# Query of head 0: from the first stage's loop to the head of the projection stream

## The chip, the cores and the metric

The kernel runs on one core of one Trainium2 chip. The metric is the time of one execution in device microseconds; below, the profile of one execution stands beside the median of three timed runs.

## The reference

One trunk layer over 512 latent tokens of width 1024, with 256 context tokens ahead of them. It is cut here to what the change touches:

```
mod = silu(c) @ w_ada + b_ada                       # six parts: shift, scale, gate, twice
h   = rmsnorm(x) * g * (1 + scale) + shift          # for latent and context tokens
z   = h @ w_in + b_in                               # x, B, C | q, k, v, r, low-rank decays | gates A, B
o   = gated linear attention over heads 0..3, forwards and backwards (q, k, v, decays)
y   = sigmoid(gate_a) * conv branch + sigmoid(gate_b) * (rmsnorm(o) * silu(r)) @ w_gla_out
x   = x + gate1 * (y @ w_o)
x   = x + gate2 * relu(h2 @ w_up)^2 @ w_down        # h2 is x, normalized and modulated again
out = rmsnorm(x)
```

The query of a head is 128 of the columns of `z`. With eight blocks of 128 input channels it is a sum over eight products; in this kernel each product of two f32 matrices is made of three matmuls on rounded halves (`mm3`, line 137: high x high, high x low, low x high).

## The kernel before

Weights are loaded as f32 into raw buffers (line 106; `NRAW` is 4, of 512 KB each), and `split` (ACT casts the high half, DVE subtracts to get the low half) fills a pair of `hi` and `lo` tiles, five pairs in rotation. `weights` (line 126) does both for one block.

**The first stage** (lines 421 to 464) runs over the eight channel blocks, called steps 0 to 7 here. A step needs the shift and scale of its block, which themselves come from a product: `ada_raw` (line 186) loads 1 MB of `w_ada` for a block in two raw buffers (four DMAs on SP), `mod_products` makes 16 small matmuls of them (`ps_mod`), ACT copies the result (`sm`), four tiny matmuls turn it into columns (`ps_mc`), and DVE adds biases (`mod`). Four transposes bring the tokens of the block to channels by tokens (`ps_xt`); ACT scales and shifts them twice, once rounded (`hh`) and once not (`h_f`), and DVE takes the difference (`hl`). Then come the products of the step: 12 matmuls for the keys of four heads (`ps_k`, weights `wk` of 256 KB, split into `wkh` and `wkl`) and three for the query of head 0 (`ps_q0`). The sums stay in PSUM over all eight steps: four banks for the keys, one for the low-rank decays, one for this query; two of the eight banks are left for `ps_mod`, `ps_mc` and `ps_xt`. `ps_mod` of a step is computed in the step before it, and the loads run two steps ahead. The query's weights take one raw buffer and one pair of `hi` and `lo` at the start of the stage (line 429).

**The steady stream** follows. `Stream` (line 531) holds a plan of weight blocks in the order of use and loads up to three ahead of the one in use, five pairs at most. `projections` (line 891) takes them: eight blocks for the values (`ps_v`, six groups of 24 matmuls for each half, with the context's tokens, keys and decays in between), then the query of head 1, the convolution's inputs and the other queries, the gates. Attention runs interleaved with it: `all_attention` is advanced once for each `yield` of `projections`; it waits for `q_t[h]`, and first starts after the first `yield`, which stands behind the first group of `ps_v`.

**What sets the order.** In the set-up, before line 431, instructions of ACT, DVE and TensorE keep the order in which they are written. In the loop and the stream a planner orders the instructions of each engine by their priority (their place in the program, with parts moved up by `tc.high_priority`) and by when it thinks that their inputs and buffers are ready. Each engine then runs its list in order. DMAs of weights are issued by SP, in one list as well, so a load that waits for a raw buffer holds up all loads behind it.

The profile names tiles without numbers at the end; `ps_q0` appears there as `ps_q`, `ps_k0` to `ps_k3` as `ps_k`, the tiles of line 429 as `r_q`, `h_q` and `l_q`.

Of the kernel before, what the change touches and what calls it, by code (L numbers as in the profile page):

```python
# [20 lines left out]
KT = D // P  # L21
# [29 lines left out]
def hybrid_block_kernel(  # L51
# [40 lines left out]
    def blk(name, dt=F32):  # L92
        return bp.tile([P, 512], dt, tag="blk", name=name)
# [9 lines left out]
    def psum(name):  # L103
        return pp.tile([P, 512], F32, tag="ps", name=name)
# [21 lines left out]
    def weights(name, src):  # L126

        raw = raw_tile("r_" + name)
        a, b = src.shape[1], src.shape[2]
        nc.sync.dma_start(out=raw.rearrange("p (a b) -> p a b", a=a), in_=src)  # L130
        hi = wp.tile([P, 1024], F32R, tag="hi", name="h_" + name)
        lo = wp.tile([P, 1024], F32R, tag="lo", name="l_" + name)
        split(raw, hi, lo, name == "up")
        latest[0] = lo
        return hi.rearrange("p (a b) -> p a b", a=a), lo.rearrange("p (a b) -> p a b", a=a)

    def mm3(ps, lh, ll, rh, rl, start, stop, late=False, more=False):


        pe.matmul(ps, lh, rh, start=start, stop=False, skip_group_check=more)  # L140
        for l, r in ((ll, rh), (lh, rl)) if late else ((lh, rl), (ll, rh)):
            pe.matmul(ps, l, r, start=False, stop=stop and r is (rl if late else rh), skip_group_check=more)

    def cols(w, c0, n=P):
        return w[:, c0:c0 + n].rearrange("(k p) c -> p k c", p=P)

    def rows(w, k0, c0):
        return w[k0 * P:(k0 + 2) * P, c0:c0 + 512].rearrange("(k p) c -> p k c", p=P)
# [272 lines left out]
    warm(5)  # L421
    ps_k = [psum(f"ps_k{h}") for h in range(HEADS)]
    ps_lr = psum("ps_lr")
    ps_q0 = psum("ps_q0")
    latent_h(0, pst)
    key_raws[1] = key_raw(1)
    mod_w[1] = [ada_raw(1, q) for q in range(2)]
    normalized(x_tok, r_x, 0, P)
    wq = weights("q0", cols(w_in, C_Q))
    key_weights(1)  # L430
    Engine.ordered = False
    for m in range(MT):
# [2 lines left out]
    for k in range(KT):  # L435
        if k == 3:
            constants()
        if k + 2 < KT:
            key_raws[k + 2] = key_raw(k + 2)
            mod_w[k + 2] = [ada_raw(k + 2, q) for q in range(2)]  # L440
            key_weights(k + 2)
        elif k + 2 == KT:
            for m in range(MC):
                t = (blk(f"c_{m}_0"), blk(f"c_{m}_1"))
                for hf in range(2):
                    nc.sync.dma_start(out=t[hf], in_=ctx[m * P:(m + 1) * P, hf * 512:(hf + 1) * 512])
                c_tok.append(t)
        st, sp_ = k == 0, k == KT - 1
        if k % 4 == 3:
            low_rank_products(ps_lr, h_f32, k - 3)  # L450
        if k == KT - 1:
            lr_parts = low_rank_parts(ps_lr, SEQ)
        for h in range(HEADS):
            if h == (k == 0) and k + 1 < KT:
                sm = mod_rows(k + 1)
            if h == 2 and 0 < k < KT - 1:
                with tc.high_priority(offset=60):
                    mod_cols(k + 1, sm)
                    latent_h(k + 1)
            mm3(ps_k[h], wk[k][0][:, h * P:(h + 1) * P], wk[k][1][:, h * P:(h + 1) * P], h_hi[k], h_lo[k], st, sp_, st)  # L460
        mm3(ps_q0, wq[0][:, k, :], wq[1][:, k, :], h_hi[k], h_lo[k], st, sp_)
        if k == 0:
            with tc.high_priority(offset=60):
                mod_cols(1, sm)
                latent_h(1)
# [87 lines left out]
            self.live -= 1  # L553
            self.pump()

    plan = [("v", rows(w_in, 2 * g, C_V + 512 * hf)) for hf in range(2) for g in range(KT // 2)]
    plan.append(("q", cols(w_in, C_Q + DK)))
    for j in range(KT):
        plan += [("xa", cols(w_in, C_XA + j * P)), ("c", cols(w_in, C_C + j * P)), ("b", cols(w_in, C_B + j * P))]
# [34 lines left out]
    v_lat = [[None, None] for _ in range(MT)]  # L594
    v_ctx = [[None, None] for _ in range(MC)]
    lr_lat = low_rank("l", low_rank_sum(lr_parts, SEQ), SEQ)
    q_t[0] = blk("q_0")
    dve.tensor_scalar(out=q_t[0], in0=ps_q0, scalar1=cb(24), scalar2=float(DK) ** -0.5, op0=ALU.add, op1=ALU.mult)
    for h in range(HEADS):
        k_lat.append(blk(f"k_{h}"))  # L600
        act.activation(out=k_lat[h], in_=ps_k[h], func=AF.Identity, bias=cb(28 + h))
# [287 lines left out]
    ya, gate, gb, og = [], [], [], []  # L889

    def projections():

        for hf in range(2):
            vb = blk(f"vb_{hf}")
            nc.gpsimd.dma_start(out=vb, in_=b_in[C_V + 512 * hf:C_V + 512 * hf + 512].partition_broadcast(P))
            wv = [ws.take("v") for _ in range(KT // 2)]
            for m in range(MT + MC):
                if hf == 0 and m == 2:
                    context_h()
                if hf == 0 and m == MT:  # L900
                    ps = psum("ps_lrc")[:, 0:CTX]
                    for k0 in (0, 4):
                        low_rank_products(ps, c_f32, k0)
                    lr_parts_c = low_rank_parts(ps, CTX)
                    for h in range(HEADS):
                        ps = psum("ps_kc")[:, 0:CTX]
                        for k in range(KT):
                            mm3(ps, wk[k][0][:, h * P:(h + 1) * P], wk[k][1][:, h * P:(h + 1) * P], c_hi[k], c_lo[k], k == 0, k == KT - 1)
                        if h % 2 == 0:
                            kb = blk(f"kc_{h}")  # L910
                        k_ctx.append(kb[:, CTX * (h % 2):CTX * (h % 2) + CTX])
                        act.activation(out=k_ctx[h], in_=ps, func=AF.Identity, bias=cb(28 + h))
                        if h == 0:
                            lr_ctx.append(low_rank("c", low_rank_sum(lr_parts_c, CTX), CTX))
                        if h % 2 == 0:
                            yield
                ps = psum("ps_v")
                for k in range(KT):
                    hh, hl = (h_hi[k], h_lo[k]) if m < MT else (c_hi[k], c_lo[k])
                    ms = slice((m % MT) * P, (m % MT + 1) * P)  # L920
                    mm3(ps, hh[:, ms], hl[:, ms], wv[k // 2][0][:, k % 2, :], wv[k // 2][1][:, k % 2, :], k == 0, k == KT - 1)
                    if m == MT + MC - 1 and k % 2:
                        ws.free()
                vt = (kblk if m < MT else blk)(f"v_{m}_{hf}")
                dve.tensor_tensor(out=vt, in0=ps, in1=vb, op=ALU.add)
                (v_lat if m < MT else v_ctx)[m % MT][hf] = vt
                yield

        def query(h):
            ps = project("q")  # L930
            q_t[h] = blk(f"q_{h}")
            dve.tensor_scalar(out=q_t[h], in0=ps, scalar1=cb(24 + h), scalar2=float(DK) ** -0.5, op0=ALU.add, op1=ALU.mult)

        query(1)
        yield
        for j in range(KT):
            xa = blk("xa")
            ps = project("xa")
            act.activation(out=xa, in_=ps, func=AF.Identity, bias=cb(j))
            yield  # L940
            ps = project("c")
            dve.scalar_tensor_tensor(out=xa, in0=ps, scalar=cb(16 + j), in1=xa, op0=ALU.add, op1=ALU.mult)
            t = blk("cv")
            act.activation(out=t, in_=xa, func=AF.Copy, scale=cb(64 + 8 + j))
            u3 = xa.rearrange("p (r w) -> p r w", w=GRID_W)
            t3 = t.rearrange("p (r w) -> p r w", w=GRID_W)
            dve.scalar_tensor_tensor(out=t3[:, :, 1:], in0=u3[:, :, :-1], scalar=cb(64 + j), in1=t3[:, :, 1:], op0=ALU.mult, op1=ALU.add)
            dve.scalar_tensor_tensor(out=t3[:, :, :-1], in0=u3[:, :, 1:], scalar=cb(80 + j), in1=t3[:, :, :-1], op0=ALU.mult, op1=ALU.add)
            yield
            ps = project("b")  # L950
            dve.scalar_tensor_tensor(out=t, in0=ps, scalar=cb(8 + j), in1=t, op0=ALU.add, op1=ALU.mult)
            new = kblk if j in (5, 6) else blk
            ya.append((new(f"yah_{j}", F32R), new(f"yal_{j}", F32R)))
            split(t, *ya[j])
            yield
            if j in (1, 4):
                query(2 if j == 1 else 3)
                yield
        for j in range(KT):
            ps = project("ga")  # L960
            gate.append(blk("ga"))
            act.activation(out=gate[j], in_=ps, func=AF.Identity, bias=cb(48 + j))
            yield
        for j in range(KT):
            pinned(act.activation(out=gate[j], in_=gate[j], func=AF.Sigmoid))
        pinned(nc.scalar.preload_act_table_set(TABLES))
        for j in range(KT):
            ps = project("co", ya)
            dve.tensor_tensor(out=gate[j], in0=gate[j], in1=ps, op=ALU.mult)
            yield  # L970
# [464 lines left out]
```

## Time and profile before

| what | us |
|---|---|
| median of 3 runs | 957.09 |
| lowest and highest run | 956.73, 957.37 |
| the profiled execution, whole | 959.36 |
| its span, first to last instruction | 957.6 |
| TensorE busy | 940.1 (98%) |
| VectorE (DVE) busy | 710.2 (74%) |
| ScalarE (ACT) busy | 536.2 (56%) |
| GpSimd (POOL) busy | 164.8 (17%) |
| mean granted TensorE clock | 0.996 of full |

Times in views are microseconds from the span's start unless marked otherwise. Matmuls overlap: a 128x512 matmul is listed with 389 ns from issue to end, but in a dense row one starts every 228 ns or so, and it is the distance between starts that counts. A wait is put down to what released the instruction last.

### The profile page before, as it was taken

The page shows a single profiled execution, that of the slowest core. Times are in us where ns is not written, and L with a number is a line of the kernel's source. Part 1 is how long each engine was busy: PE and PEld are TensorE (multiplying, and loading weights), DVE is VectorE, ACT ScalarE, POOL GpSimd, SP SyncE. Part 2 cuts the span into 40 slices and gives each one's busy share as a digit, 9 for nine tenths or more (in the row PEclk, how much of TensorE's full clock was granted, in tenths as well). Part 3 has the DMA queues.
Part 4 walks back from the last instruction along what each step waited for, and adds up shares of the span by engine and source line. Part 5 has one row for each costly group of instructions (what it writes and reads, how often), then busy time and mean ns, then how long its engine had stood idle before and what let it go on. Part 6 is the DMA issues. An engine that isn't in the chain of part 4 may idle for free.

```text
span 957.6 us, 14834 instructions
## 1 busy us (share of the span) xinstructions
PE 940.1 (98%) x5555; PEld 800.1 (84%) x5555; DVE 710.2 (74%) x1170; ACT 536.2 (56%) x1008; POOL 164.8 (17%) x231
## 2 busy tenths in 40 slices
PE   6999999999999999999999999999999999999996
PEld 4678888788888888888888888899999998888886
DVE  5366685888598859977566484688768778899896
ACT  5476453745565556743543332478777687656662
POOL 8011022132112200002000000122445540000000
PEclk9999999999999999999999999999999999999999
DMA  9784072989648843636538466322557859655661
GB/s 288 225 293 169 5 250 74 233 188 192 172 132 215 172 120 103 206 98 181 184 95 261 130 216 202 130 88 63 189 169 177 188 128 309 227 191 190 196 220 44
DMA packets 162040, 165.51 MB, mean 173 GB/s; under 512 B 7524, under 2 KB 126416, under 8 KB 161712
## 3 DMA queue, kind: packets, MB, share of 16 engines
q1 hardware_dynamic: 147248, 124.94, 43.3%
q0 software_dynamic: 13568, 37.53, 15.9%
q10 hardware_dynamic: 1152, 2.10, 0.6%
q8 instruction: 43, 0.70, 0.3%
q14 instruction: 29, 0.24, 0.1%
HBM read 160.35 MB, written 37.75 MB: 207 GB/s over the span
## 4 chain that ended last, share of the span: by engine, by line
PE 91%; DVE 3%; DMA 3%; ACT 1%; issue 1%; SPq 0%; POOL 0%; DVEq 0%; POOLq 0%; ACTq 0%
PE ps_ua L83 8%; PE ps_da L83 7%; PE ps_v L83 6%; PE ps_c L83 5%; PE ps_ga L83 5%; PE ps_b L83 5%; PE ps_xa L83 5%; PE ps_r L83 5%; PE ps_y L83 5%; PE ps_db L83 5%; PE ps_gb L83 5%; PE ps_go L83 5%; PE ps_uc L83 4%; PE ps_co L83 4%; PE ps_dc L83 2%; PE ps_k L83 2%
## 5 line engine op out<-in xcount | busy, mean ns | idle before, releaser
L83 ACT CAST h_dn<-r_dn 128x1024 fp32r<-128x1024 f32 x56 | 59.0, 1054 | 48.0 <-PE ps_da L83 20.5
L83 DVE TENSOR_TENSOR l_dn<-r_dn,h_dn 128x1024 fp32r<-128x1024 f32 x56 | 68.1, 1221 | 14.7 <-ACT h_dn L83 14.4
L83 PE MATMUL ps_da<-h_dn,ap 128*128 128x512 f32 x192 | 59.6, 389 | 0.0
L83 DVE SCALAR_TENSOR_TENSOR acc<-wa,silu_c,acc 128x512 f32<-128x512 f32 x64 | 45.8, 747 | 12.4 <-DMA wa<-in_w_ada_dram 10.1
L83 PEld LDWEIGHTS ps_da<-h_dn,ap 128*128 128x128 f32 x192 | 36.0, 188 | 7.5
L486 POOL DMA_DIRECT2D t<-in_w_down_dram x48 | 40.3, 864 | 4.0 <-issue 3.9
L83 PE MATMUL ps_db<-h_dn,ap 128*128 128x512 f32 x128 | 39.8, 389 | 0.0
L83 PE MATMUL ps_da<-l_dn,ap 128*128 128x512 f32 x96 | 37.3, 389 | 0.0
L83 DVE TENSOR_TENSOR ap<-ug,ap 128x512 fp32r<-128x512 f32 x56 | 36.2, 685 | 0.0
L514 POOL TENSOR_TENSOR r_up<-r_up,r_up 128x512 f32<-128x512 f32 x14 | 24.3, 1737 | 48.3 <-DVE r_up L83 42.8
L83 ACT CAST ap<-ug 128x512 fp32r<-128x512 f32 x56 | 31.9, 617 | 0.3 <-DVE t_n L83 0.3
L1067 POOL DMA_DIRECT2D x<-x x8 | 4.4, 545 | 155.1 <-DVE x L83 152.3
L83 PEld LDWEIGHTS ps_db<-h_dn,ap 128*128 128x128 f32 x128 | 24.0, 188 | 4.9
L510 POOL TENSOR_TENSOR r_up<-r_up,r_up 128x512 f32<-128x512 f32 x14 | 25.9, 1852 | 6.2 <-DMA r_up<-in_w_up_dram 6.2
L83 PE MATMUL ps_v<-h_v,hh 128*128 128x512 f32 x64 | 25.8, 403 | 0.0
L83 PE MATMUL ps_xa<-hh,h_xa 128*128 128x512 f32 x64 | 25.5, 398 | 0.0
L83 PE MATMUL ps_ga<-hh,h_ga 128*128 128x512 f32 x64 | 25.4, 397 | 0.0
L83 PE MATMUL ps_b<-hh,h_b 128*128 128x512 f32 x64 | 25.4, 396 | 0.0
L83 PE MATMUL ps_c<-hh,h_c 128*128 128x512 f32 x64 | 25.3, 396 | 0.0
L83 PE MATMUL ps_co<-yah,h_co 128*128 128x512 f32 x64 | 25.2, 394 | 0.0
L83 PE MATMUL ps_r<-hh,h_r 128*128 128x512 f32 x64 | 25.1, 392 | 0.0
L83 PE MATMUL ps_y<-h_wo,yh 128*128 128x512 f32 x64 | 25.1, 392 | 0.0
(526 smaller groups left out, 3391.3 us busy)
## 6 DMA issues: line engine op xcount, KB each, us to landing
t<-in_w_down_dram POOLq DMA_DIRECT2D x48, 512.0 KB, 7.9
wa<-in_w_ada_dram SPq DMA_DIRECT2D x32, 512.0 KB, 4.1
r_up<-in_w_up_dram SPq DMA_DIRECT2D x32, 512.0 KB, 4.2
r_dn<-t SPq DMA_DIRECT2D x32, 512.0 KB, 4.1
r_dn<-in_w_down_dram SPq DMA_DIRECT2D x24, 512.0 KB, 4.4
wa<-in_w_ada_dram SPq DMA_DIRECT2D x32, 256.0 KB, 4.7
t<-t POOLq DMA_DIRECT2D x16, 512.0 KB, 5.6
r_v<-in_w_in_dram SPq DMA_DIRECT2D x8, 512.0 KB, 5.0
```

The source lines that it names most:

```text
L83: ins = op(*args, **kwargs)
L486: pinned(nc.gpsimd.dma_start(out=t_sum[i][p], in_=src, **({"accum_op": ALU.add} if add else {})))
L510: pinned(nc.gpsimd.tensor_tensor(out=b0, in0=a0, in1=b0, op=ALU.add))
L514: pinned(nc.gpsimd.tensor_tensor(out=a0, in0=b1, in1=a0, op=ALU.subtract))
L1067: nc.gpsimd.dma_start(out=x1_d[m][:, hf, :], in_=x1[m][hf])
```

## The change

The query of head 0 leaves the loop: its PSUM bank, its weights and its three matmuls of each step, and the operation on DVE behind the loop that adds the bias and scales. It becomes the first entry of the stream's plan and is computed by the same function as the other queries, `query(0)`, as 24 matmuls in one group ahead of the first values, without a `yield` behind it.

```diff
@@ -421,12 +421,10 @@
     ps_lr = psum("ps_lr")
-    ps_q0 = psum("ps_q0")
     latent_h(0, pst)
...
     normalized(x_tok, r_x, 0, P)
-    wq = weights("q0", cols(w_in, C_Q))
     key_weights(1)
...
             mm3(ps_k[h], wk[k][0][:, h * P:(h + 1) * P], wk[k][1][:, h * P:(h + 1) * P], h_hi[k], h_lo[k], st, sp_, st)
-        mm3(ps_q0, wq[0][:, k, :], wq[1][:, k, :], h_hi[k], h_lo[k], st, sp_)
...
-    plan = [("v", rows(w_in, 2 * g, C_V + 512 * hf)) for hf in range(2) for g in range(KT // 2)]
+    plan = [("q", cols(w_in, C_Q))]
+    plan += [("v", rows(w_in, 2 * g, C_V + 512 * hf)) for hf in range(2) for g in range(KT // 2)]
...
     lr_lat = low_rank("l", low_rank_sum(lr_parts, SEQ), SEQ)
-    q_t[0] = blk("q_0")
-    dve.tensor_scalar(out=q_t[0], in0=ps_q0, scalar1=cb(24), scalar2=float(DK) ** -0.5, op0=ALU.add, op1=ALU.mult)
...
     def projections():
+        def query(h):
+            ps = project("q")
+            q_t[h] = blk(f"q_{h}")
+            dve.tensor_scalar(out=q_t[h], in0=ps, scalar1=cb(24 + h), scalar2=float(DK) ** -0.5, op0=ALU.add, op1=ALU.mult)
+
+        query(0)
...
-
-        def query(h):
-            ps = project("q")
-            q_t[h] = blk(f"q_{h}")
-            dve.tensor_scalar(out=q_t[h], in0=ps, scalar1=cb(24 + h), scalar2=float(DK) ** -0.5, op0=ALU.add, op1=ALU.mult)
 
         query(1)
         yield
```

## Rows read from the trace of the kernel before

**Rows 1.** Waits of TensorE, whole span: total us, times, longest us.
```profile
PE ps_mod L83 <- DMA wa<-in_w_ada_dram: 1.4, 2, 0.7
PE ps_mc L83 <- ACT sm L83: 0.5, 1, 0.5
```

**Rows 2.** The chain of waits: start us, length us, what; first stage, and a later query.
```profile
23.65 6.13 DMA wa<-in_w_ada_dram
29.78 0.14 issue
29.91 0.67 PE ps_mod L83 x8
...
31.09 0.61 PE ps_mc L83 x4
...
32.19 3.06 PE ps_k L83 x8
35.25 0.82 PE ps_q L83 x2
...
45.93 1.00 PE ps_mod L83 x16
...
51.45 1.00 PE ps_mod L83 x16
...
208.53 5.44 PE ps_q L83 x24
```

**Rows 3.** Stretches of the first stage: each engine's busy us, TensorE's clock, DMA share, GB/s.
```profile
22.00:30.00 8.00, 7.25 (x61) 4.98 (x63) 2.95 (x8) 4.11 (x7) 2.10 (x2) 1.00 1.02 299
31.95:35.90 3.95, 3.95 (x14) 3.12 (x13) 2.01 (x5) 3.06 (x5) 0.00 (x0) 0.57 1.04 322
36.00:42.00 6.00, 6.00 (x44) 3.86 (x43) 2.96 (x6) 0.98 (x3) 0.00 (x0) 1.00 0.02 7
50.00:68.00 18.00, 18.00 (x111) 12.40 (x110) 11.99 (x26) 12.88 (x23) 1.13 (x2) 1.00 0.95 324
```

**Rows 4.** Issues on SP in order of time: start us, us, what, count.
```profile
14.43 0.43 SPq L130 DMA_DIRECT2D r_q<-in_w_in_dram  x1
...
23.22 0.93 SPq L191 DMA_DIRECT2D wa<-in_w_ada_dram  x2
...
27.64 1.59 SPq L191 DMA_DIRECT2D wa<-in_w_ada_dram  x2
...
52.08 0.88 SPq L130 DMA_DIRECT2D r_v<-in_w_in_dram  x2
```

**Rows 5.** TensorE, ACT and DVE in order of time: start us, us, what.
```profile
20.11 1.05 ACT L83 CAST h_q<-r_q 128x1024 fp32r<-128x1024 f32 x1
21.19 1.22 DVE L83 TENSOR_TENSOR l_q<-r_q,h_q 128x1024 fp32r<-128x1024 f32 x1 [0.36 <-ACT h_q L83]
23.71 0.39 PE L83 MATMUL ps_q<-hh,h_q 128*128 128x512 f32 x1
...
28.20 0.40 PE L83 MATMUL ps_q<-hh,h_q 128*128 128x512 f32 x1
28.53 0.64 PE L83 MATMUL ps_mod<-wa,silu_w 128*32 128x256 f32 x8
...
46.00 0.69 DVE L83 TENSOR_TENSOR hl<-h_f,hh 128x512 fp32r<-128x512 f32 x1
47.21 0.40 PE L83 MATMUL ps_k<-hl,wkh 128*128 128x512 f32 x1
49.57 0.62 ACT L83 CAST wkh<-wk 128x512 fp32r<-128x512 f32 x1 [2.14 <-DMA wk<-in_w_in_dram]
51.57 0.69 DVE L83 TENSOR_TENSOR hl<-h_f,hh 128x512 fp32r<-128x512 f32 x1 [0.66 <-ACT h_f L83]
52.72 0.40 PE L83 MATMUL ps_k<-hl,wkh 128*128 128x512 f32 x1
```

**Rows 6.** DMA issues, first 80 us: count, KB each, median us to landing.
```profile
wa<-in_w_ada_dram SPq DMA_DIRECT2D x32, 256.0 KB, 4.7
r_v<-in_w_in_dram SPq DMA_DIRECT2D x8, 512.0 KB, 5.0
r_q<-in_w_in_dram SPq DMA_DIRECT2D x2, 512.0 KB, 5.7
```

## The prediction

> **What bounds the kernel now.** I read four views, in this order. First the waits of TensorE over the whole span [rows 1]: behind its start-up the only entries of any size that the change could touch are the wait for a `w_ada` load (the second of two, 0.7 us) and the 0.5 us for the copy `sm`. All else is matmul after matmul. So the end of the kernel is the sum of TensorE's work, and a change can only move it by removing work, gaps, or slow matmuls. Second the chain of waits around the first stage [rows 2]: it is DMA until 29.78, then nothing but TensorE, through `ps_k`, `ps_v` and on. Third the stretches [rows 3]: between 22 and 36 us the DMA engines are full (a share of 1.02, and 1.04 at the end of it), TensorE has gaps, and from 31.95 to 35.90 its granted clock averages 0.57, most of it at 1.2 GHz; from 36 to 42 the DMA engines stand still (0.02), because the next load waits for a raw buffer that only the next `ps_mod` sets free; then TensorE is full. Fourth the issues on SP [rows 4] and the order of TensorE, ACT and DVE in the stage [rows 5], to see which load stands before which matmul.
>
> All durations are of the profiled execution: 957.6 us span, 959.36 us in all. The median of the runs is 957.09, 2.27 less; I carry differences over to it unchanged.
>
> **The change part by part.**
>
> *The matmuls that move.* Twenty-four `ps_q` matmuls leave the loop, three in each of eight steps, and the same 24 stand before the first `ps_v` group. A later query of the same shape took 5.44 us for 24 [rows 2], 0.227 us each; three are 0.68 in the loop. Both ends are TensorE at its limit, so the move itself is 0. The bias-and-scale on DVE moves along and is read by attention only behind the first `ps_v` group, in both programs; the cover for it, a group of 24 matmuls, stays.
>
> *The load that moves.* The query weights are 0.52 MB, issued at 14.43 in front of the loads of steps 2 and 3 [rows 4]. At the 299 GB/s of 22 to 30 us [rows 3] that is 1.75 us of a full DMA. It also held one of four raw buffers until the DVE split `l_q` ended at 22.4 [rows 5], and the second half of step 3's load, issued from 23.22 on, reused that very buffer. That load landed at 29.78, and TensorE waited for it from 29.17, where the first eight `ps_mod` of row 28.53 end, to 29.91 [rows 2, 5]: 0.74 us. Without the query load it lands at about 28.03. TensorE comes there earlier too, because four `ps_q` matmuls (first 23.71, last 28.20, rows 5; 0.91 us) are gone: 28.26. So the wait ends, worth **0.74 us**. Below, nothing is gained if the issue is held by buffers anyway; above, the 0.54 us wait of `ps_mc` for `sm` could go as well (1.28). I take 0.74, which is the row of this very wait; behind it the chain `sm`, `ps_mc` is late next, and I leave its 0.54.
>
> *The low clock.* Ten matmuls behind that stall took 3.06 + 0.82 = 3.88 us [rows 2] against 10 x 0.228 = 2.28 at 2.4 GHz: **1.60 us** lost. Before the clock fell, TensorE had stood idle 0.74 and 0.54 us within two microseconds. With the first gone I take it that the clock stays up; the other end is that it falls all the same (0). I take 1.60 because TensorE had small gaps at other times between 20 and 29 us too (7.25 us busy of 8, most of the missing part after 29) and the clock there stayed at 1.00 [rows 3].
>
> *Shorter steps.* From 40 us on a step lasts 5.5 us (45.93 to 51.45, rows 2) and gets 0.68 shorter. What the `ps_q` matmuls covered is the path from a step's `ps_xt` over `hh` and `h_f` to `hl`. In step 4 `hl` ends at 46.69 and its first matmul starts at 47.21: 0.52 us of slack, 0.16 short of 0.68. In step 5 ACT cast the key weights `wkh` of step 6 first, for whose load it waited 2.14 us until 49.57; behind it came `hh`, `h_f`, and `hl` ended at 52.26 with its first matmul at 52.72 [rows 5]: 0.46 of slack. That load was released two steps before the matmul by a `ps_mod`, so there the need comes 2 x 0.68 = 1.36 earlier: 0.90 short. No later step was as close. The cost is 0.16 + 0.90 = **1.05 us**, if ACT keeps that order. From below it is 0 (ACT does `hh` before the cast), from above 2.04 (three steps stay as long as they are). I take 1.05, since it comes from the rows themselves.
>
> *The load, and its split, at the new place.* SP now issues the query weights behind the last `w_ada` and key loads and ahead of the values; on that queue it is moved past all loads of steps 2 to 7. The first value loads were issued at 52.08 [rows 4], in the raw buffer that becomes free with the `ps_mod` of step 6. Put there, the query takes 5.7 us to land like before [rows 6], plus 1.05 on ACT and 1.22 on DVE [rows 5]: ready at 60.1. The loop, shorter by three times 0.68 from there on, ends at 64.9. 4.8 us of slack. The fourth value load now waits for the buffer of the query: 60.1, plus 5.0 [rows 6] and 2.3 for the same steps, 67.4, and it is needed some 4 us into `ps_v`, at 64.9 + 5.44 + 4 = 74. So both are hidden; if the DMA share of 0.95 from 50 to 68 [rows 3] delays them by more than their slack, each microsecond beyond costs one. GpSimd's sums of `w_down` hang on the splits of the values, as before, and move with them: 0. The PSUM bank given back (six of eight were held through the loop) removes no wait that the rows show: 0 from this alone.
>
> *Sum.* 959.36 - 0.74 - 1.60 + 1.05 = 958.07, a gain of 1.29. On the median: 957.09 - 1.29 = **955.8 us**.
>
> **A rule that speaks against it.** The row: between 29.17 and 31.09 TensorE did 0.67 us of work, and behind that its clock fell to 0.57 of full [rows 2, 3, 5]. The Trainium skill (TensorE: Matmul & The Clock Gate, "HAM oscillation — how this bites in real kernels") says that a loop whose matmuls are shorter than the DMA wait for its next slice sinks to the slow clock at every slice, and advises more matmul work per slice; by it, three matmuls fewer in each step leave the low stretch where it is, which is rival 2. The trace agrees at the one place where a load is late, and not in the steps after 42 us, where the engine stays full.
>
> **The rivals.**
>
> 1. *The early part closes up further.* The program's order is made anew by a planner; with no split of query weights on ACT and DVE at 20 to 22.4 us, `ps_k` of step 1 may stand ahead of the third `ps_mod`. Then 0.54 goes as well, and if ACT also puts `hh` ahead of the late cast, the 1.05: gain 0.74 + 1.60 + 0.54 = 2.9, 954.2. For it: two spare PSUM banks become three. Against: the order shown put `ps_mod` first, and the loads remain full to 36 us.
>
> 2. *The low stretch stays.* A gap of 0.54 us for `sm` is left, and 0.91 us of filling work is gone. Gain 0.74, loss 1.05: 957.4. For it: TensorE loses work exactly where loads set the pace. Against: its waits shrink from 1.28 to 0.54.
>
> 3. *Slower: the wait moves on to step 4.* The third `ps_mod` already ran ahead of most `ps_k` of step 1. With fewer matmuls and a third spare bank the planner can run a `ps_mod` further ahead, before the keys of steps 1 and 2. The last piece of step 4's load is the second of the two issues of row 27.64 [rows 4], at 28.67; with the median 4.7 us to land [rows 6] it lands at 33.4, or 31.6 without the query load. TensorE, with 1.65 us saved, would reach that `ps_mod` right behind the `ps_xt` that ended at 32.19, at 30.5: a wait of 1.1, and up to 2.9 if the load is not earlier. The low stretch stays and, after a longer wait, repeats (+1.60). With -0.74 and +1.05: +1.4 to +4.8, about 960.0. It decides from the point where that `ps_mod` stands before more than some 5 of the 20 `ps_k` that now precede it.
>
> That the change doesn't do what it says I rule out: the products are the same 24.
>
> **How the numbers follow.** The forecast has 0.43 (its own range, from gains of 0.3 to 2.4, gives 0.08 of that to a gain over 1.91), rival 1 0.25, rival 2 0.13, rival 3 0.19. A measurement tells about 0.2%, 1.91 us, from no change. Faster by more: 0.08 and nearly all of rival 1, **0.32**. Slower by more: rival 3 but for its mildest form, **0.18**. Within: **0.50**. The range reaches from rival 1 with ACT's order and some further gaps closed (a gain of 3.8 is all that TensorE's gaps and low clock between 20 and 36 us hold) to rival 3 at its middle: **953.3 to 959.8**, leaving out less than 0.2.
>
> **What would show it.** A right first step: no wait of `ps_mod` for `wa` near 29 us, and the landing of the second half of step 3's load about 1.7 us earlier. A right second: granted clock 1.00 from 30 to 36 us. A right third: matmuls on `hl` of steps 4 and 5 that wait 0.2 and 0.9 us for DVE, and steps of 4.8 us otherwise. A right fourth: `ps_q` dense in about 5.45 us ahead of `ps_v`, no wait for `h_q` or `l_q`. Wrong would be waits for `wa` at a later step, a second low stretch, or any new wait behind the first `ps_v`.

## The result, and the profile after

The changed kernel takes 963.73 us (median of 5 runs, 962.91 to 964.27) against 957.09 before: 1.0069 times as long, 95% interval 1.0054 to 1.0084, 6.6 us slower. The forecast was 955.8 with a range of 953.3 to 959.8. The profiled execution took 962.91, its span is 961.1. The two profiled executions are only 3.55 us apart: the one before lay 2.27 over its median, the one after 0.82 under.

**Where the time is.** The chain of waits of the changed kernel (start us, length us, what), from the first low-rank matmul to the values; it answers to [rows 2]:

```profile
33.22 0.97 PE ps_lr L83 x2
...
36.24 0.99 PE ps_lr L83 x4
37.24 0.90 PE ps_mod L83 x12
...
41.92 1.00 PE ps_mod L83 x16
...
44.89 1.00 PE ps_mod L83 x16
45.89 0.84 PE ps_lr L83 x2
...
50.53 0.55 PE ps_mod L83 x2
...
53.13 0.99 PE ps_mod L83 x14
...
55.23 0.98 PE ps_lr L83 x2
...
61.46 0.99 PE ps_lr L83 x2
...
62.47 0.59 ACT lrp L83
...
63.11 1.12 PE ps_lrs L83 x2
64.24 1.85 PE ps_k L83 x8
66.08 5.45 PE ps_q L83 x24
71.54 5.44 PE ps_v L83 x24
```

The same chain before, the rows of it that name these tiles (two more of `ps_mod`, at 45.93 and 51.45, stand in [rows 2]):

```profile
39.57 0.99 PE ps_lr L83 x8
40.57 0.86 PE ps_mod L83 x16
...
56.96 1.00 PE ps_mod L83 x16
...
62.48 1.00 PE ps_lr L83 x8
...
67.11 0.86 PE ps_lrs L83 x2
67.97 5.49 PE ps_v L83 x24
```

`ps_v` starts 3.57 us later, and the span ends 3.5 us later (961.1 against 957.6): all of the difference between the two traces stands ahead of `ps_v`, and nothing behind it counts. The 24 moved matmuls take 5.45 us at their new place, but the loop ends only 1.89 us earlier (66.08 against 67.97). In the loop, `ps_lr`, the low-rank decays, is the new thing: two groups before, six places after. (A low-rank matmul shows as two instructions, so x8 is a group of four and x2 is one alone. At 36.2 us three of them stand mixed with `ps_mod`.) The sixth place is not on the chain; in TensorE's list it is this:

```profile
57.16 1.05 PE L83 MATMUL ps_lr<-h_f,lr_raw 128*32 128x512 f32 x2
```

How the price comes about is seen best in the groups of TensorE's instructions over the loop (shape, count, busy us, mean ns of one, idle before). Before:

```profile
L83 PE MATMUL ps_mod<-wa,silu_w 128*32 128x256 f32 x112 | 8.3, 385 | 0.7 <-DMA wa<-in_w_ada_dram 0.7
...
L83 PE MATMUL ps_lr<-h_f,lr_raw 128*32 128x512 f32 x16 | 2.1, 604 | 0.0
```

After:

```profile
L83 PE MATMUL ps_mod<-wa,silu_w 128*32 128x256 f32 x112 | 9.6, 385 | 0.0
L83 PE MATMUL ps_lr<-h_f,lr_raw 128*32 128x512 f32 x16 | 6.3, 603 | 0.0
```

The counts and the mean of one are the same; the busy time, which counts overlapping instructions once, is not. Four matmuls with 32 columns each, written into four quarters of the partitions, ran at once when they stood together; torn apart they run one after the other at the price of four. The busy time of `ps_lr` grew by 4.2 us and that of `ps_mod`, which is built alike (in two places it too is torn, into 2 and 14 and around low-rank matmuls), by 1.3. These two must not be added: at 36 us both kinds run at once, and that stretch is in both. The chain counts each microsecond once: there `ps_lr` takes 4.77 us against 1.99, and `ps_mod` from 37 us on 4.44 against 3.86 (from 40 us on before). That is 3.4 us, and 4.4 with the lone matmul at 57.16, during which the chain stands at DVE. So of the 6.6 us, 3.4 to 4.4 are the price of the torn groups.

The waits of TensorE from 18 to 80 us, total, times, longest; they answer to [rows 1]:

```profile
PE ps_lrs L83 <- ACT lrp L83: 0.7, 1, 0.7
PE ps_mc L83 <- ACT sm L83: 0.6, 1, 0.6
PE ps_k L83 <- DVE hl L83: 0.2, 1, 0.2
```

The wait for the load is gone, as forecast; the one for `sm` stayed, as forecast; two new ones make 0.9 us. And a stretch of the changed kernel (columns as in [rows 3]):

```profile
30.00:36.00 6.00, 6.00 (x27) 3.99 (x25) 2.34 (x6) 3.20 (x5) 0.00 (x0) 1.00 0.89 269
```

The clock stays at 2.4 GHz between 30 and 36 us, where it was low in [rows 3]. This looked like a second step come true, but in this execution the low stretch lies elsewhere, in the start-up.

```profile
12.00:18.00 6.00, 5.07 (x26) 3.71 (x23) 2.31 (x11) 2.39 (x6) 5.11 (x9) 0.54 1.09 300
```

The first experiment shows the same for the kernel before.

### The profile page after: what moved, and what is told of

It is laid out like the page before. It is cut to its first block, busy times and chain, and to the rows that moved or that the text cites. A ratio compares the mean times of both kernels' runs of the same rounds, so it can differ in the third digit from the quotient of the medians.

```text
span 961.1 us, 14833 instructions
## 1 busy us (share of the span) xinstructions
PE 943.0 (98%) x5555; PEld 800.3 (83%) x5555; DVE 710.2 (74%) x1170; ACT 536.3 (56%) x1008; POOL 162.8 (17%) x231
## 4 chain that ended last, share of the span: by engine, by line
PE 92%; DVE 3%; ACT 2%; DMA 1%; issue 1%; POOL 0%; SPq 0%; DVEq 0%; POOLq 0%; ACTq 0%
PE ps_ua L83 8%; PE ps_da L83 7%; PE ps_v L83 6%; PE ps_c L83 5%; PE ps_ga L83 5%; PE ps_b L83 5%; PE ps_xa L83 5%; PE ps_r L83 5%; PE ps_y L83 5%; PE ps_db L83 5%; PE ps_gb L83 5%; PE ps_go L83 5%; PE ps_uc L83 4%; PE ps_co L83 4%; PE ps_k L83 2%; PE ps_dc L83 2%
```

## The experiments

Theory 1: the change tore the groups of low-rank matmuls apart. Theory 2: the loss is the cover that `ps_q` gave to the way to `hl` in each step. Theory 3: it is the late load of the query's weights, whose cast holds up ACT. Theory 4, for one experiment: the written order itself costs, and loads set the waits. Theory 5: it is the third spare PSUM bank. Ratios are to the kernel before, run on the same chip.

**The kernel before once more** (no edit).

> The kernel before, unchanged, profiled once more. Its profile took 959.36 us, 2.27 over the median of its timed runs. Theory A: the wait for the load near 29 us (0.74) and the low clock behind it (1.60) are an accident of that one execution, 2.34 together; then this profile takes about 957.1 and shows neither. Theory B: they belong to the program, and the 2.27 is what profiling adds; then both stand here again and the time is about 959.4.

958.52 us in one execution, span 956.7. Its stretches:

```profile
12.00:18.00 6.00, 4.61 (x27) 2.78 (x27) 1.47 (x8) 1.79 (x5) 4.65 (x9) 0.55 1.05 290
...
30.00:36.00 6.00, 5.16 (x36) 4.04 (x33) 2.66 (x6) 3.19 (x7) 0.00 (x0) 1.00 1.02 317
```

Between the theories: the wait for the load stays (0.3 us near 30 us), so does the 0.5 for `sm`, but the clock is full from 30 to 36 us although TensorE is busy only 5.16 of 6, and it is low from 12 to 18 instead. The low stretch moves from one execution to the next. Of the 2.34 us that I had counted as the program's, 1.60 were that execution's. The loop says the same. The first key matmul in the first profile, in this one and in the changed kernel:

```profile
19.01 0.40 PE L83 MATMUL ps_k<-hh,wkh 128*128 128x512 f32 x1
19.88 0.40 PE L83 MATMUL ps_k<-hh,wkh 128*128 128x512 f32 x1
18.79 0.61 PE L83 MATMUL ps_k<-hh,wkh 128*128 128x512 f32 x1
```

The first `ps_v` group of this profile, in its chain:

```profile
66.77 5.49 PE ps_v L83 x24
```

From the one to the other it is 49.0 us in the first profile (to 67.97), 46.9 here and 52.8 in the changed kernel (to 71.54). Against this second execution the loop and the moved group are 5.9 us longer, near to the 6.6 of the medians.

**Low-rank matmuls grouped** (in the changed kernel):

```diff
-        for k in range(k0, k0 + 4):
+        for k in reversed(range(k0, k0 + 4)):
             g = slice(32 * (k - k0), 32 * (k - k0) + 32)
-            pe.matmul(ps[g], lr_raw[:, k, :], h[k], start=k0 == 0, stop=k0 > 0)
+            ins = pe.matmul(ps[g], lr_raw[:, k, :], h[k], start=k0 == 0, stop=k0 > 0)
+            if h is h_f32:
+                pinned(ins)
```

> The changed kernel, with the four low-rank matmuls of each half of the loop pinned one behind the other, the latest input first. Theory 1 (the change let the planner tear the groups of four apart, and a matmul of 32 columns takes about 0.97 us alone as well as four together): six places of 0.90 to 1.06 us, 5.8 in all, become two of 0.88 and 1.0, so about 3.9 us come back: profile near 959.0, median near 959.8. Theory 2 (shorter steps: halves and weights come late): the waits stay as they are, the low-rank order is worth nothing: 963.7 within 0.9.

960.0 us, ratio 1.0017 (1.0003 to 1.0030): of 0.69% the grouping gives back 0.52, 5.0 us, with about 2 us either way by the two intervals, so the forecast of 3.9 fits. With the groups the planner also keeps `ps_mod` as whole as before (8.3 us) and sets `ps_lrs` behind the last keys. The groups and the chain in this kernel:

```profile
L83 PE MATMUL ps_mod<-wa,silu_w 128*32 128x256 f32 x112 | 8.3, 385 | 0.2 <-DMA wa<-in_w_ada_dram 0.2
L83 PE MATMUL ps_lr<-h_f,lr_raw 128*32 128x512 f32 x16 | 2.1, 604 | 0.0
```

```profile
37.56 1.00 PE ps_lr L83 x8
...
59.21 1.00 PE ps_lr L83 x8
...
63.34 5.49 PE ps_q L83 x24
68.83 5.44 PE ps_v L83 x24
```

What it still loses are two waits, 1.1 us for `hl` near 34.7 us, behind the cast of key weights whose load landed at 32.6, and 0.8 for `sm`, which stands behind the cast of the query's weights:

```profile
54.19 1.05 ACT L83 CAST h_q<-r_q 128x1024 fp32r<-128x1024 f32 x1 [1.59 <-DMA r_q<-in_w_in_dram]
55.15 0.37 ACT L83 COPY sm<-ps_mod 128x256 f32<-128x256 f32 x1
```

**Low-rank matmuls alone, in the kernel before:**

```diff
-        if k % 4 == 3:
-            low_rank_products(ps_lr, h_f32, k - 3)
-        if k == KT - 1:
-            lr_parts = low_rank_parts(ps_lr, SEQ)
         for h in range(HEADS):
+            if h == 2:
+                pinned(pe.matmul(ps_lr[32 * (k % 4):32 * (k % 4) + 32], lr_raw[:, k, :], h_f32[k], start=k < 4, stop=k >= 4))
+                if k == KT - 1:
+                    lr_parts = low_rank_parts(ps_lr, SEQ)
```

> The kernel before, query of head 0 still in the loop, but each low-rank matmul pinned into its own step instead of four together at steps 3 and 7. Theory 1: eight places of 0.97 us instead of two of 0.9 to 1.0, so about 5.9 us more: 963.0. Theory 2: TensorE hides them in gaps it has anyway: 957.1 within 0.7.

965.22 us, ratio 1.0066 (1.0043 to 1.0090). Here the query of head 0 is in the loop as before, and the loss of the change is there all the same. The eight places take 8.4 us in place of 2.1, and 0.66% is 6.3 us: the time rose by as much as the busy time.

```profile
L83 PE MATMUL ps_lr<-h_f,lr_raw 128*32 128x512 f32 x16 | 8.4, 604 | 0.0
```

**A PSUM bank held** (in the changed kernel):

```diff
     ps_lr = psum("ps_lr")
+    held = psum("ps_held")
+    pe.matmul(held, ones_r, ones_r.unsqueeze(1).to_broadcast([P, 4, P]), start=True, stop=True)
...
+    held_s = sp.tile([P, 1], F32, tag="held", name="held", bufs=1)
+    dve.tensor_copy(out=held_s, in_=held[:, 0:1])
     lr_lat = low_rank("l", low_rank_sum(lr_parts, SEQ), SEQ)
```

> The changed kernel with one PSUM bank kept occupied from the start of the loop to its end, so that two are spare as in the kernel before. Theory 5 (the third spare bank lets the planner run ahead and tear the groups): the groups are whole again, about 4 us under the changed kernel. Theory 1 (it is the room on TensorE, not the bank): six places of low-rank matmuls as in the changed kernel and the same time, 963.7, plus 0.2 for the one matmul that fills the bank.

966.96 us, ratio 1.0098 (1.0081 to 1.0116). The groups stay torn (6.5 us), so the bank is not what tears them, and theory 5 falls. That it is slower than the change itself (2 runs) was not expected by theory 1 either, which had 963.9; in the one trace `ps_mod` waits for a load near 48 us:

```profile
PE ps_mod L83 <- DMA wa<-in_w_ada_dram: 1.4, 1, 1.4
```

**Load at the old place, matmuls at the new one** (in the changed kernel; the last line of the edit to `query` uses the early weights for head 0):

```diff
     normalized(x_tok, r_x, 0, P)
+    wq = weights("q0", cols(w_in, C_Q))
     key_weights(1)
...
-    plan = [("q", cols(w_in, C_Q))]
-    plan += [("v", ...
+    plan = [("v", ...
...
-            ps = project("q")
+            ps = project("q") if h else tiles("q", h_lat, wq)
```

> The changed kernel, but the weights of the query are loaded and split where the kernel before does it, ahead of the loop; the 24 matmuls stay behind the loop, and the low-rank order is left to the planner. It puts the first group as one and three, the second whole. Theory 1 (the cost is the torn low-rank groups): one place more than before, 0.97 us, instead of four more: about 3 us under the changed kernel, 0.4% over the kernel before at most. Theory 3 (the cost is the late load: ACT holds back the copy sm behind the cast of the query's weights, as in the grouped kernel at 54 us, 0.8 us): 0.8 us under the changed kernel and no more.

961.25 us, ratio 1.0043 (1.0029 to 1.0056): 2.5 us under the changed kernel by the ratios, nearer to theory 1, though the two intervals leave room for the 0.8 of theory 3. With the splits of the query's weights on ACT and DVE ahead of the loop, the planner tears one low-rank group and not the other (3.2 us), and `ps_mod` still (9.8):

```profile
L83 PE MATMUL ps_mod<-wa,silu_w 128*32 128x256 f32 x112 | 9.8, 386 | 0.4 <-DMA wa<-in_w_ada_dram 0.4
L83 PE MATMUL ps_lr<-h_f,lr_raw 128*32 128x512 f32 x16 | 3.2, 604 | 0.0
```

So it is the whole changed schedule, the work on ACT and DVE too, that decides what the planner tears.

**The same with the groups pinned** (this edit and that of the grouped kernel).

> The grouped changed kernel (0.17% over the kernel before) with the load and split of the query's weights at the old place, ahead of the loop. What is left to explain in the grouped kernel are waits of 1.1 us for hl of step 2 and 0.8 us for sm behind the cast of the query's weights. Theory 3 (the late load costs 0.8): that wait goes, the one of 0.3 to 0.7 for a load of w_ada near 29 us comes back: about 0.1 to 0.2% over the kernel before. Theory 2 (all that is left is the cover): unchanged at 0.2%.

959.1 us, ratio 1.0022 (1.0009 to 1.0034). The wait for a load is back (1.0 us near 29 us), as theory 3 has it. The wait for `sm` near 55 us shrinks from 0.8 to 0.3 us but does not go: the cast of the first value weights now stands where that of the query's stood.

```profile
53.19 1.05 ACT L83 CAST h_v<-r_v 128x1024 fp32r<-128x1024 f32 x1 [1.18 <-DMA r_v<-in_w_in_dram]
54.14 0.37 ACT L83 COPY sm<-ps_mod 128x256 f32<-128x256 f32 x1
```

The time does not tell this kernel from the grouped one.

**Late load, split behind the loop's work on ACT** (in the grouped kernel; the plan and `query` as in the edit before the last):

```diff
-        split(raw, hi, lo, name == "up")
+        split(raw, hi, lo, name in ("up", "q0"))
...
+    wq = weights("q0", cols(w_in, C_Q))
     t_sum = [[dp.tile([P, 2, 512], F32, tag=f"t{i}_{p}", name=f"t{i}_{p}") for p in range(NFF // 4)] for i in range(4)]
```

> The grouped changed kernel, with the query's weights still loaded late but the split pinned behind the loop's last work on ACT, so that the copy sm of step 7 doesn't stand behind the cast. Theory 3: 0.8 us less than the grouped kernel, 0.05 to 0.12% over the kernel before, with no wait of ps_mc for sm near 55 us. Theory 2: the 0.8 us is covered elsewhere and the time stays at 0.17% over.

958.79 us, ratio 1.0014 (1.0004 to 1.0023). In the trace the wait near 55 us is gone, but the interval overlaps those of the two kernels above: theory 3 is seen as a wait and not settled as time. Its runs spread from 956.6 to 960.4.

**TensorE in the written order**, first in the grouped changed kernel, then in the kernel before:

```diff
-                if Engine.ordered:
+                if Engine.ordered or (Engine.pe_ordered and self.engine is nc.tensor):
                     tc.keep_in_program_order(ins)
...
     Engine.ordered = False
+    Engine.pe_ordered = True
...
+    Engine.pe_ordered = False
     t_sum = [[dp.tile([P, 2, 512], F32, tag=f"t{i}_{p}", name=f"t{i}_{p}") for p in range(NFF // 4)] for i in range(4)]
```

> The changed kernel with TensorE's instructions in the loop pinned in the order in which they are written (low-rank groups of four together, each group of ps_mod whole, one step after the other). Theory 1: what the change lost is order; with it restored the change costs nothing, and what the early load gave back stays: 956 to 957.5. Theory 2: in shorter steps the halves hl come 0.2 to 0.9 us late in several steps, whatever the order: 958.5 to 961, with waits of ps_k for DVE hl in the trace.

964.51 us, ratio 1.0060 (1.0036 to 1.0083), theory 2 and beyond (it had 958.5 to 961): with whole groups, but steps in strict order, it is as slow as the change. Its waits:

```profile
PE ps_k L84 <- DVE hl L84: 3.3, 2, 2.8
PE ps_lr L84 <- ACT h_f L84: 0.8, 1, 0.8
```

> The kernel before with TensorE's loop pinned in written order, the same order as the pinned changed kernel (0.60% over the kernel before, waits for hl 3.3 us and for h_f 0.8 us), but with the three matmuls of the query in each step. Theory 2 (in that order it is the filling by the query's matmuls that covers the way to hl): those waits shrink by up to 0.68 us for each step that has one, 4.1 to about 2 us, and the time is 0.3 to 0.4% over the kernel before. Theory 4 (the written order itself is what costs, and loads set the waits): the waits stay at about 4 us and the time at 0.6% over.

960.16 us, ratio 1.0027 (1.0011 to 1.0043). The same order with the query's matmuls in it:

```profile
PE ps_k L84 <- DVE hl L84: 2.0, 1, 2.0
```

The waits went from 4.1 to 2.0 us and the ratio from 0.60 to 0.27%, about as theory 2 said for this order, though the two intervals just overlap (from 0.36%, up to 0.43%). So in the written order the matmuls of `ps_q` cover waits. Not all of the 2.1 us need be cover: the longest wait, 2.8 and 2.0 us, stands in both traces behind key weights, and these landed 7.7 us after the first key matmul in one (27.37 and 19.69) and 7.1 in the other (25.97 and 18.83). Both executions also have their low clock in the loop, between 28 and 36 us. In the grouped kernel, in the planner's own order, the wait for `hl` is 1.1 us.

**The query in the loop, from step 2 on** (in the kernel before; its load at line 429 goes):

```diff
             key_weights(k + 2)
+            if k == 1:
+                wq = weights("q0", cols(w_in, C_Q))
...
-        mm3(ps_q0, wq[0][:, k, :], wq[1][:, k, :], h_hi[k], h_lo[k], st, sp_)
+        for i in ((), (), (0,), (1, 2), (3,), (4, 5), (6,), (7,))[k]:
+            mm3(ps_q0, wq[0][:, i, :], wq[1][:, i, :], h_hi[i], h_lo[i], i == 0, i == KT - 1)
```

> The kernel before with the query of head 0 still in the loop, but its weights loaded two steps later and its eight products spread over steps 2 to 7 (one, two, one, two, one, one), nothing pinned. The planner leaves both low-rank groups whole. Theory 1 (the loss of the change is the torn groups and the lost filling, the gain is the load out of the full early DMA): the wait of 0.3 to 0.7 us for a load of w_ada near 30 us goes, nothing else comes, 0.3 to 0.7 us under the kernel before. Theory 2 (the query's matmuls are also needed in steps 0 and 1): waits for sm and hl near 30 us grow by up to the 1.4 us of those six matmuls, 0.5 to 1 us over.

957.6 us, ratio 1.0001 (0.9992 to 1.0009), the same as before. Both groups stay whole without a pin. The wait for the load is gone, and one of 0.5 us for `hl` has come:

```profile
PE ps_mc L83 <- ACT sm L83: 0.6, 1, 0.6
PE ps_k L83 <- DVE hl L83: 0.5, 1, 0.5
```

So taking the load out of the early stage brought nothing that can be measured; what its wait alone is worth is not separated from the new wait for `hl`. No version beats the kernel before.

## Why the prediction was wrong

- **"The move itself is 0"**: right for the matmuls that move (5.45 us for 24, 5.44 expected). The step failed in what it left out. It treated the other instructions of the loop as if they kept their order, although the same text said in rival 1 that the order is made anew. The grouped matmuls of `ps_lr` were in no term of the sum; the trace before had them as two pieces x8 of 0.99 and 1.00 us and, in the list by form, 16 matmuls of 604 ns in 2.1 us busy, a factor of four and a half in overlap to be lost. That term stood at nothing; with `ps_mod` it measured 3.4 to 4.4 us in the trace of the change. Undone it gives some 5 us back (3 to 7 by the intervals), and put into the kernel before it costs 0.66%: that is shown.
- **The load wait, 0.74**: the mechanism was right. The wait near 29 us is gone in the changed kernel. Its size was off: 0.7 in one execution of the kernel before, 0.3 in the other, and without the load but with the query still in the loop the time is the same (1.0001), with a wait of 0.5 us for `hl` in its place.
- **The low clock, 1.60**: wrong term. It belonged to the one execution that I read, as the second one shows. The profiled execution was 2.27 us over the median, and to carry the difference over unchanged was the mistake: a stretch that the median may not hold cannot be saved from it. The step from the waits to the clock ("with the first gone I take it that the clock stays up") is not borne out either: with the early load and the groups pinned, TensorE waited 0.96 and 0.54 us at the same place, and the clock from 30 to 36 us was 1.00, after a low stretch at 12 to 20.
- **Shorter steps, 1.05**: the mechanism (ACT casts weights whose load is late ahead of `h_f`, and `hl` comes late) shows in the grouped kernel, 1.1 us, but in step 2 and not in 4 and 5. In the changed kernel there is one wait for `hl`, 0.2 us at 58.4, in the last step, where ACT had waited for `ps_xt` and not for a load.
- **The load at its new place, 0**: its slack was there (no wait for `h_q` or `l_q`), but its place in SP's list was not the one assumed, 52.08 behind the last key load. In the changed kernel it and a value load go ahead of the last key load:

```profile
45.52 0.37 SPq L130 DMA_DIRECT2D r_q<-in_w_in_dram  x1
46.00 1.13 SPq L130 DMA_DIRECT2D r_v<-in_w_in_dram  x1
47.19 0.92 SPq L207 DMA_DIRECT2D wk<-in_w_in_dram  x1
```

  And its cast stands in ACT's list ahead of a copy that the loop needs. That is a wait of 0.8 us in the grouped kernel, which the times did not resolve. I asked when the weights are needed, not what is queued behind their cast.
- **The bank, 0**: holding it did not mend the groups, so it is not the cause.
- **Rival 3**, the slower side at 0.18, had the right agent (the planner runs work ahead on a TensorE with more room) and the wrong victim: `ps_mod` waiting for loads. Such a wait at a later step showed only in the kernel with the bank held (1.4 us near 48 us).
- **Rival 2**, the low stretch that stays, decided nothing: TensorE had less work per load, and the clock from 30 to 36 us was 1.00, with the low stretch at 12 to 19 us.

The Trainium skill (TensorEngine Tiling (Array Packing), "Key Properties") says that tiles of the array operate independently and can run weight loads and matmuls in parallel. The traces agree: four matmuls of 32 columns take 1.00 us together and 0.97 alone.

What stays open: why the planner tears these groups exactly when the query leaves. Filling on TensorE from step 2 on keeps them whole, and so in part does the early split; a model of its decisions was not made. The rest of the 6.6 us, some 2 to 3 beside the 3.4 to 4.4 of the groups, I put down in part to the two new waits of 0.9 us and to the way to `hl` in the last step, from one trace: argued and not tested apart. With the groups whole 0.17% remains.

## What to carry to other kernels

When a planner orders the instructions, a change to one set of matmuls re-orders the others, so look first for groups that are cheap only while they stand together, and pin them. The sign of such a group is a busy time far below count times mean: here 2.1 us for 16 x 604 ns, a factor of 4.5, where a plain dense row has 1.7 (24 x 389 ns in 5.45 us). And do not add the busy times of two kinds that can overlap each other; the chain of waits counts each microsecond once. And before a gap of one profiled execution is counted as a gain, compare that execution with the median, or profile again.

## What the runs showed of the hardware

One 128x32 matmul over 512 f32 columns costs TensorE 0.97 us alone, and four of them in different quarters of the output's partitions 1.00 us together. The stretch of low clock, 1.2 GHz, was at 32 to 36 us in one execution of the kernel before and at 12.5 to 19.5 us in another; in the first it cost 1.60 us of matmuls, in the second it fell on the start-up. Of the twelve profiled executions nine show one such stretch in their first 80 us, six of them between 12 and 20 us and three between 28 and 36, and three show none.
